# Even and odd partitions for attention's q and k loads, later counted times for the delta rule's loads, and six other order weights

## The chip, the cores and the metric

The kernel runs on one core of one Trainium2 chip. The metric is the device time of one launch in microseconds (us), the median of several runs; a profile is one more execution with the hardware profiler on. TensorE is called PE below, VectorE DVE, ScalarE ACT, GpSimd POOL, and SyncE, which issues all the transfers spoken of here, SP.

## The reference, cut to what matters

One layer of a mixer: 1024 latent tokens and 256 context tokens of width 1024 are normalised, projected once by a wide matrix, and go through two branches. Branch A is a gated delta rule over chunks, in both directions of the sequence, with 8 heads; branch B is differential softmax attention with 8 heads, each with two score maps. Both are gated, projected, merged and projected again.

```python
def gdn_chunk_scan(q, k, v, g, beta, s0, with_out):
    ...
    def step(s, xs_i):
        u_i, w_i, kd_i, gl_i = xs_i[:4]
        v_new = u_i - jnp.einsum('bhck,bhkv->bhcv', w_i, s)
        s_next = s * jnp.exp(gl_i)[..., None, None] + jnp.einsum('bhck,bhcv->bhkv', kd_i, v_new)
        if with_out:
            qd_i, qk_i = xs_i[4:]
            o = jnp.einsum('bhck,bhkv->bhcv', qd_i, s) + jnp.einsum('bhij,bhjv->bhiv', qk_i, v_new)
            return s_next, o
    ...

def diff_attend(q, k, v, lam):
    ...
    def block(qi):
        s = jnp.einsum('bqhcd,bkhcd->bhcqk', qi, k).astype(jnp.float32) * scale
        p = jax.nn.softmax(s, axis=-1)
        attn = p[:, :, 0] - lam * p[:, :, 1]
        return jnp.einsum('bhqk,bkhv->bqhv', attn.astype(v.dtype), v)
    ...

def mixer_output(...):
    ...
    merged = g_a * (y_a.reshape(b, length, GDN_WIDTH) @ w_oa) + g_b * (y_b.reshape(b, length, DIFF_V_WIDTH) @ w_ob)
    return merged @ w_out
```

## The kernel before, in words

**Stages.** By the span of the profile: modulation and the normalised input (0 to about 150 us); the input projection with the convolution and the delta rule's triangular matrices (to about 745 us); the scan of the delta rule, with the rest of the projection between its steps (to about 1290 us); a short stretch in which the projection ends and attention begins (to about 1345 us); attention, with the product by `w_oa` in its gaps (to about 1790 us); then the product by `w_ob`, the merge and `w_out`.

**How the order is set.** All work is written as generators, called streams here. Each yields the engine of its next instruction, the time counted for it, what it depends on, and the call that emits it. When the kernel is built, `flow` and `turn_flow` keep a counted clock for each engine, and emit the instruction that by these clocks could start first; in attention a number for each kind of stream, the table `ABIAS`, decides among those that could start within `TOL` = 0.02 us of each other on one engine, and the scores, the turns, the value products and the merge also have counted due times (`due`). What is emitted first stands first in its engine's queue, so the counted times fix the order on all five engines; on the chip each engine goes through its queue in that order, and waits where an input is not there. `later(t, us)` adds microseconds to the counted time of a finished item and emits nothing.

**The scan.** For each head h of 8 and each direction d of 2, ten tiles of 128 tokens (two chunks each) are gone through one after the other. A step has the products `chain` (with `vv`, or with `S,sk` for the state S; with `r,x`; with `vd,kk`) and two products `out`. `sets` loads four tiles for each head, on SP: `vv`, `kk`, `sk` and `sq` (512 to 640 KB each). `loads` fetches `x` for two steps at a time (256 KB), and POOL masks half of it (`tqk`). Between the steps stand `mm` (products of the input projection, 128x512), `gram` and the small triangular products `pz`, `pu`.

**Attention.** For each head, `att_load_ops` loads `qh` (high part of q) and `kk`, and `att_low_ops` loads `ql` (low part of q). Each of these tiles has 128 partitions by 2 rows; the 128 partitions are filled by two transfers, s = 0 and s = 1, of 64 partitions each, and `kk`'s two come from two different arrays (`kd[0]`, `kd[1]`). The scores `s` contract over the partitions, so that q and k have to agree on which partition holds what, and nothing else does. For each block of 128 queries, 64 in all: `s` is 12 products (`s<-kk,qh`, `s<-kk,ql`) into banks that DVE empties (`S`, L1560) with a running minimum; ACT takes the exponential (L1573); POOL and ACT scale and add the two maps (L1592, L1590, L1597); PE turns the map, ten transposes `t<-ct,S` (L63) in groups of 4, 4 and 2; ACT and DVE split what was turned into a high and a low part (`ah` L1629, `al` L1634), and empty the banks with that; PE multiplies by the values (`v<-ah,vh` and so on, 30 products of 256 columns for two blocks). `osq`, `oT` and `rr` belong to the head's norm; `rr<-rbd` comes back through memory before POOL (L1720) can scale `oT`. `merge` is the stream of the products `ma` (128x512), 16 groups of 24; each group's end is multiplied by a gate `g` (L1806), which SP loads ahead (`g<-gt`, L1791).

SP issues its transfers in its own queue's order, and the transfers share the core's DMA engines. All of PE's products have line L56, its transposes L63.

Of the kernel before, what the change touches and what calls it, by code (L numbers as in the profile page):

```python
# [8 lines left out]
F32 = mybir.dt.float32  # L9
# [8 lines left out]
P = 128  # L18
# [16 lines left out]
PE, DVE, ACT, POOL, DMA, ADMA, DV2, PL1 = range(8)  # L35
# [8 lines left out]
class Block:  # L44
# [193 lines left out]
    def front(self, st, early, kv0):  # L238
# [190 lines left out]
        for g, b in ((loads(), 0), (modulation(), 1), (smalls(), 1), (rms(), 2), (weights(), 1.5), (turns(), 1), (self.forever(turnq[0]), 1.2),  # L429
                     (self.forever(turnq[1]), 1.2), (main(), 9)):  # L430
            self.stream(g, b)
# [822 lines left out]
    def sets(self):  # L1254

        nc = self.nc
        free = []
        for h in range(H):
            yield lambda: self.gs and min(self.scanned) >= h and self.tailed >= h - 1
            w = dict(seen={}, oa=self.gs.tile([P, NL, P], F32, tag=f"oa{h % 2}", name="oa"))  # L1260
            free = [self.over, self.ready[h - 1]["tail"] if h else None]
            for n, src in (("vv", self.gv[h]), ("kk", self.gkk[h]), ("sk", self.gkq[h][:, :LT]), ("sq", self.gkq[h][:, LT:])):
                if h == 0 and n == "kk":
                    yield lambda: all((d, 0, 8) in self.units_ for d in range(2))
                w[n] = self.gs.tile([P, L] if n == "sq" else [P, NT, P] if n in ("kk", "vv") else [P, LT], F32, tag=n, name=n)
                w["t" + n] = yield DMA, 1.82, free, lambda: nc.sync.dma_start(
                    w[n], src.rearrange("(c p) f -> p c f", p=P) if n in ("kk", "vv") else src)
            self.ready[h] = w

    def loads(self, d):  # L1270

        nc, i = self.nc, 0
        order = ((8, 0, 2, 4, 6), (8, 6, 4, 2, 0))[d]
        for h in range(H):
            for c in order:
                yield lambda: self.gs and self.stored > h and len(self.used_[d]) > i - 2
                x, e = self.gs.tile([P, 2, 2, P], F32, tag=f"x{d}", name="x", bufs=2), 2 if c < NL else 1
                u = dict(x=x[:, 0], qk=x[:, 1])
                u["tx"] = yield DMA, 0.45 * e, [self.store_t[h], self.used_[d][i - 2] if i > 1 else None], \
                    lambda: nc.sync.dma_start(x[:, :e], self.xq[h][:, d, c // 2, :e])  # L1280
                if c < NL:
                    u["tqk"] = yield POOL, 0.72, [self.later(u["tx"], 1.0)], lambda: nc.gpsimd.tensor_tensor(
                        x[:, 1], x[:, 1], (self.up, self.lo)[d].unsqueeze(1).to_broadcast([P, 2, P]), ALU.mult)
                self.units_[d, h, c] = u
                i += 1
# [145 lines left out]
    def named(self, n, gen):  # L1431
        s = self.entry[n] = [gen, self.ABIAS.get(n, 0), None, None]
        s[2] = next(gen, None)
        self.streams.append(s)

    def due(self, n, i):

        self.entry[n][1] = self.ABIAS.get(n, 0) + self.DUE * i

# [48 lines left out]
    def att_load_ops(self, h):  # L1488

        q, pool, tags = self.nc.sync, self.a0 if h % 2 else self.gh[0], ("qh", "kk") if h % 2 else ("kq", "X")  # L1490
        w = self.aT[h] = dict(qh=pool.tile([P, 2, L], F32R, tag=tags[0], name="qh"),
                              kk=pool.tile([P, 2, LT], F32R, tag=tags[1], name="kk"))
        old = self.seen_.get(h - 2)
        w["t"] = []
        for s in range(2):
            d, v = slice(64 * s, 64 * s + 64), lambda x: x.rearrange("(c d) n -> d c n", c=2)
            w["t"] += [(yield DMA, 1.46, [old], lambda: q.dma_start(w["qh"][d].bitcast(F32), v(self.qd[0, h]))),
                       (yield DMA, 1.82, [old], lambda: q.dma_start(w["kk"][d].bitcast(F32), v(self.kd[s, h])))]

    def att_low_ops(self, h):  # L1500

        w = self.aT[h]
        w["ql"] = self.a0.tile([P, 2, L], F32R, tag=f"ql{h % 2}", name="ql")
        w["tl"] = []
        for s in range(2):
            w["tl"].append((yield DMA, 1.46, [self.seen_.get(h - 2)], lambda: self.nc.sync.dma_start(
                w["ql"][64 * s:64 * s + 64].bitcast(F32), self.qd[1, h].rearrange("(c d) n -> d c n", c=2))))

    def att_heads(self):
        for h in range(H):  # L1510
# [219 lines left out]
    def side_start(self):  # L1730
# [10 lines left out]
    ONACT = (1, 2, 3)  # L1741
    TOL = 0.02
    PACE = 4.48
    ABIAS = dict(rels=-0.59, softs=8.84, norms=5.82, gateq=-27.29, sums=-14.54,
                 outs=-42.85, lows=-2.4, highs=-9.33, adds=26.02, scales=31.0, evs=22.29, mouts=-3.31,
                 att_out=8.18, turns=3.19, scores=-12.11, merge=1.0)
    KEEP = 3

    def side_values(self):
# [453 lines left out]
```

## Time and profile before

| | |
|---|---|
| runs before | 1964.64, 1964.72, 1966.32 us; median 1964.72 |
| the profiled execution | 1966.57 us, of which the span is 1964.8 us |
| PE busy | 1909.4 us, 97% of the span |
| DVE, ACT, POOL busy | 75%, 54%, 34% |
| PE busy in the scan, 745 to 1290 us | 530.3 of 545 us |
| PE busy in the start of attention, 1290 to 1400 us | 102.4 of 110 us |
| PE busy in attention, 1400 to 1790 us | 383.0 of 390 us; DVE 333.5, ACT 304.3 |

Busy time on PE says that PE had a matmul in flight, not that it ran at its best rate. PEclk is the granted clock of PE, 1.00 at full rate. A view of waits names, for each engine, what ended a stretch in which it had nothing to do; a view by windows gives the busy time of each engine, the granted clock and the DMA engines' busy share in stretches of the span. The chain of waits goes back from the last instruction to whatever released each one.

### The profile page before, as it was taken

The numbers are of one execution on the slowest core, as the hardware profiler recorded it, in microseconds if no ns is written. First come the engines' busy times: TensorE is split into PE (matmuls) and PEld (weight loads), VectorE is DVE, ScalarE is ACT, GpSimd is POOL, SyncE is SP. The second block draws the span as 40 slices with busy tenths as digits, with TensorE's granted clock in tenths as the row PEclk, the third lists the DMA queues.
The fourth block names the chain that finished last, engine by engine and source line by source line (L and its number), as shares of the span: only waits on it lengthen the run. The fifth ranks groups of instructions, "written<-read, shape, count | busy, mean of one in ns | idle before, by whom it ended". The sixth has DMA issues, their size and how long they took to land.

```text
span 1964.8 us, 37491 instructions
## 1 busy us (share of the span) xinstructions
PE 1909.4 (97%) x13807; PEld 1679.4 (85%) x13807; DVE 1465.1 (75%) x3613; ACT 1069.4 (54%) x2191; POOL 677.4 (34%) x610
## 2 busy tenths in 40 slices
PE   6999999999999999999999999999999999999999
PEld 4988888899999998888888888877888888888887
DVE  4687998948877987778777673336688979895677
ACT  4543445335325464767755745456687868884222
POOL 3200000005431332343433234233666757762203
PEclk9999999999999999999999999999999999999999
DMA  9144544674546557866777466585566684426542
GB/s 329 60 132 107 144 94 114 145 220 140 183 132 211 150 191 207 257 208 211 249 217 248 114 221 214 153 202 159 159 161 151 156 230 132 129 87 209 182 155 86
DMA packets 383038, 336.39 MB, mean 171 GB/s; under 512 B 142609, under 2 KB 323443, under 8 KB 381831
## 3 DMA queue, kind: packets, MB, share of 16 engines
q1 hardware_dynamic: 382855, 333.99, 57.4%
q8 instruction: 109, 1.79, 0.4%
q14 instruction: 74, 0.61, 0.1%
HBM read 222.14 MB, written 111.79 MB: 170 GB/s over the span
## 4 chain that ended last, share of the span: by engine, by line
PE 77%; DVE 8%; DMA 7%; ACT 3%; issue 2%; SPq 1%; POOL 1%; DVEq 0%; ACTq 0%; POOLq 0%
PE mm L56 38%; PE s L56 6%; PE v L56 6%; PE chain L56 5%; PE mb L56 5%; PE ma L56 4%; PE x L56 3%; PE t L63 3%; PE out L56 2%; DVE S L1560 1%; PE gram L56 1%; DMA vv<-gv 1%; DVE ac L595 1%; PE pz L56 1%; DMA g<-gt 1%
## 5 line engine op out<-in xcount | busy, mean ns | idle before, releaser
L56 PE MATMUL mm<-hs,wh 128*128 128x512 f32 (+1 forms) x2048 | 648.2, 390 | 1.5 <-DVE hs L408 1.4
L56 PEld LDWEIGHTS mm<-hs,wh 128*128 128x128 f32 x2048 | 371.9, 190 | 60.8 <-issue 2.7
L56 PE MATMUL mm<-hs,wl 128*128 128x512 f32 (+1 forms) x1024 | 398.4, 389 | 1.1 <-issue 1.1
L56 PE MATMUL mm<-wh,hs 128*128 128x256 f32 (+1 forms) x1792 | 332.7, 286 | 0.3 <-ACT sq L977 0.3
L56 PEld LDWEIGHTS mm<-wh,hs 128*128 128x128 f32 x1792 | 280.7, 191 | 0.8 <-ACT sq L977 0.5
L1560 DVE TENSOR_SCALAR_CACHE_REDUCE S<-s,rsq 128x512 f32<-128x512 f32 (+1 forms) x384 | 241.4, 656 | 29.4 <-PE s L56 25.9
L56 PE MATMUL mm<-wl,hs 128*128 128x256 f32 (+1 forms) x896 | 255.6, 285 | 0.0
L56 PEld LDWEIGHTS mm<-hs,wl 128*128 128x128 f32 x1024 | 194.4, 190 | 28.7 <-issue 0.9
L1597 POOL TENSOR_TENSOR S<-S 128x1280 f32<-128x1280 f32 x64 | 188.6, 2954 | 78.0 <-ACT S L1590 77.1
L1573 ACT ACTIVATE S<-S,mn 128x1280 f32<-128x1280 f32 x128 | 175.3, 1371 | 44.9 <-DVE mn L1572 43.2
L56 PEld LDWEIGHTS mm<-wl,hs 128*128 128x128 f32 x896 | 171.3, 191 | 0.1
L595 DVE SCALAR_TENSOR_TENSOR ac<-xc,convT,ac 128x1284 f32<-128x1284 f32 (+1 forms) x96 | 138.8, 1449 | 11.9 <-ACT ac L593 11.2
L56 PE MATMUL s<-kk,qh 128*128 128x512 f32 (+1 forms) x384 | 144.5, 376 | 2.9 <-DVE S L1560 2.9
L56 PE MATMUL s<-kk,ql 128*128 128x512 f32 (+1 forms) x384 | 134.0, 359 | 2.5 <-DMA ql<-qd 2.5
L1634 DVE TENSOR_TENSOR al<-t,ah 128x512 fp32r<-128x512 f32 (+1 forms) x192 | 109.5, 596 | 29.8 <-ACT ah L1629 28.9
L1629 ACT CAST ah<-t 128x512 fp32r<-128x512 f32 (+1 forms) x192 | 91.9, 518 | 32.6 <-PE t L63 15.3
L580 POOL MEMSET xc<- 128x2 f32 (+1 forms) x64 | 3.6, 101 | 297.8 <-ACT sq L629 113.6
L63 PE MATMUL t<-ct,S 128*128 128x128 f32 x640 | 98.6, 277 | 4.1 <-DVE al L1634 2.6
L1157 DVE TENSOR_TENSOR ts<-ts,tmp 80x31 f32<-80x31 f32 (+15 forms) x248 | 97.5, 393 | 6.1
L1318 ACT ACTIVATE vd<-chain,edk 128x128 f32<-128x128 f32 x144 | 52.3, 370 | 89.2 <-PE chain L56 83.7
L1155 DVE TENSOR_TENSOR tmp<-ab,ts 80x31 f32<-80x31 f32 (+15 forms) x248 | 94.5, 381 | 8.5 <-DMA ab<-da 3.0
L56 PE MATMUL v<-ah,vh 128*128 128x256 f32 x320 | 93.0, 291 | 0.0
(296 smaller groups left out, 4338.3 us busy)
## 6 DMA issues: line engine op xcount, KB each, us to landing
wr<-in_w_in_dram SPq DMA_DIRECT2D x48, 512.0 KB, 6.0
hx<-in_w_in_dram SPq DMA_DIRECT2D x64, 256.0 KB, 6.4
x<-xq SPq DMA_DIRECT2D x64, 256.0 KB, 3.8
X<-gcd SPq DMA_DIRECT2D x8, 1280.0 KB, 8.3
kd<-col SPq DMA_DIRECT2D x40, 256.0 KB, 2.2
xq<-X SPq DMA_DIRECT2D x16, 640.0 KB, 7.4
kk<-kd SPq DMA_DIRECT2D x16, 640.0 KB, 7.9
kq<-gkq SPq DMA_DIRECT2D x8, 1152.0 KB
```

The source lines that it names most:

```text
L56: self.nc.tensor.matmul(out, lhsT, rhs, start=start, stop=stop)
L63: self.nc.tensor.transpose(out, src, self.ident[:src.shape[0], :src.shape[0]])
L580: x["e"].append((yield PL1, 0.1, [old], lambda: nc.gpsimd.memset(xc[:, a:b], 0.0)))
L595: t = yield DV2, 1.21e-3 * wd, [t], lambda: nc.vector.scalar_tensor_tensor(ac[:, :wd], xc[:, j:j + wd], self.convw(j, x["ct"]), ac[:, :wd] ...
L1155: t = yield DV2, n * w / 960.0 + 0.08, [t if j else self.later(t, 2.5), t1], lambda: V.tensor_tensor(tv, ab[:, j + 1:, j:j + 1].to_broadca ...
L1157: t = yield DV2, n * w / 960.0 + 0.08, [t, t1], lambda: V.tensor_tensor(ts[:, j + 1:, :w], ts[:, j + 1:, :w], tv, ALU.subtract)
L1318: td = yield ACT, 0.251, [t], lambda: nc.scalar.activation(vd, pc[:, 1], AF.Copy, scale=self.edk[:, c, g:g + 1])
L1560: e = yield DVE, 0.675 if m == 512 else 0.408, [e, self.sfree[c].get(n - 4 + c)], lambda: self.nc.vector.tensor_scalar(x["S"][c][:, o:o + ...
L1573: x["x"].append((yield ACT, 1.36, [e], lambda: nc.scalar.activation(S, S, AF.Exp, bias=x["mn"][:, c:c + 1], scale=-1.0, accum_out=w["l0"][ ...
L1597: e = yield POOL, 2.9, [e], lambda: self.nc.gpsimd.tensor_tensor(S0, S0, S1, ALU.add)
L1629: e = yield ACT, 0.48 if nb == 4 else 0.27, [t, y["old", k]], lambda: self.nc.scalar.copy(y["ah", k][:, :, q], pv)
L1634: t = yield DVE, 0.603 if k < 2 else 0.322, [e, y["old", k]], lambda: self.nc.vector.tensor_tensor(y["al", k][:, :, q], pv, y["ah", k][:, ...
```

## The change

It has three parts. (1) `att_load_ops` and `att_low_ops`: the two transfers of `qh`, `kk` and `ql` write the even partitions (s = 0) and the odd ones (s = 1), where before they wrote partitions 0 to 63 and 64 to 127. The number of transfers, their sizes and what is read from memory stay. (2) `sets` counts the end of each of its four loads 1.3 us later, and `loads` counts the end of each `x` load 1.0 us later for all who use it (before, for the mask on POOL alone). (3) Six numbers of the table `ABIAS` are other ones. Parts 2 and 3 emit nothing; they and the redrawn counted clocks put the same instructions into another order, from about 745 us of the span on. Before that place, and in the products by `w_ob` and `w_out`, PE's order is the one of before.

```diff
@@ sets @@
                 w["t" + n] = yield DMA, 1.82, free, lambda: nc.sync.dma_start(
                     w[n], src.rearrange("(c p) f -> p c f", p=P) if n in ("kk", "vv") else src)
+                w["t" + n] = self.later(w["t" + n], 1.3)
             self.ready[h] = w
@@ loads @@
                 u["tx"] = yield DMA, 0.45 * e, [self.store_t[h], self.used_[d][i - 2] if i > 1 else None], \
                     lambda: nc.sync.dma_start(x[:, :e], self.xq[h][:, d, c // 2, :e])
+                u["tx"] = self.later(u["tx"], 1.0)
                 if c < NL:
-                    u["tqk"] = yield POOL, 0.72, [self.later(u["tx"], 1.0)], lambda: nc.gpsimd.tensor_tensor(
+                    u["tqk"] = yield POOL, 0.72, [u["tx"]], lambda: nc.gpsimd.tensor_tensor(
@@ att_load_ops @@
         for s in range(2):
-            d, v = slice(64 * s, 64 * s + 64), lambda x: x.rearrange("(c d) n -> d c n", c=2)
+            d, v = slice(s, P, 2), lambda x: x.rearrange("(c d) n -> d c n", c=2)
@@ att_low_ops @@
             w["tl"].append((yield DMA, 1.46, [self.seen_.get(h - 2)], lambda: self.nc.sync.dma_start(
-                w["ql"][64 * s:64 * s + 64].bitcast(F32), self.qd[1, h].rearrange("(c d) n -> d c n", c=2))))
+                w["ql"][s:P:2].bitcast(F32), self.qd[1, h].rearrange("(c d) n -> d c n", c=2))))
@@ weights @@
-    ABIAS = dict(rels=-0.59, softs=8.84, norms=5.82, gateq=-27.29, sums=-14.54,
-                 outs=-42.85, lows=-2.4, highs=-9.33, adds=26.02, scales=31.0, evs=22.29, mouts=-3.31,
-                 att_out=8.18, turns=3.19, scores=-12.11, merge=1.0)
+    ABIAS = dict(rels=-0.59, softs=8.84, norms=5.82, gateq=-27.29, sums=-18.71,
+                 outs=-21.73, lows=-2.4, highs=-9.33, adds=36.19, scales=31.0, evs=22.29, mouts=-3.31,
+                 att_out=1.9, turns=3.19, scores=-21.22, merge=25.46)
```

The order moves at three places that matter below. The first is PE at the first head of the scan: `gram` is a product of the keys and queries, `mm` one of the input projection, and `chain<-vv,x` the first step of a head, which needs the load `vv`. Before:

```order
L56 MATMUL gram<-kq 128x128 x4
L56 MATMUL mm<-hs,wl 128x512
L56 MATMUL mm<-hs,wh 128x512 x2
L56 MATMUL mm<-hs,wl 128x512
L56 MATMUL chain<-vv,x 128x128 x2
L56 MATMUL mm<-hs,wh 128x512 x2
```

The same place in the changed kernel:

```order
L56 MATMUL gram<-kq 128x128 x4
L56 MATMUL mm<-hs,wl 128x512
L56 MATMUL mm<-hs,wh 128x512 x2
L56 MATMUL mm<-hs,wl 128x512
L56 MATMUL mm<-hs,wh 128x512 x2
L56 MATMUL mm<-hs,wl 128x512
L56 MATMUL mm<-hs,wh 128x512 x2
L56 MATMUL mm<-hs,wl 128x512
L56 MATMUL chain<-vv,x 128x128 x2
L56 MATMUL gram<-kq 128x128 x4
L56 MATMUL mm<-hs,wh 128x512 x2
L56 MATMUL chain<-vd,kk 128x128 x2
```

Six `mm` more stand ahead of the first `chain<-vv,x`, and four `gram` and two `mm` between it and `chain<-vd,kk`.

The second place is SP's queue at the first `ql` loads of attention, between the last weight tiles of the projection (`hx`), the gates' store (`gt<-zo`) and the values (`vh`, `vl`). Before:

```order
L1405 DMA ya<-oa 128x512
L880 DMA hx<-in_w_in_dram 128x4x128 x2
L1506 DMA ql<-qd 64x2x1024 x2
L1525 DMA vh<-vd 128x4x128
L1525 DMA vl<-vd 128x4x128
```

The same place in the changed kernel:

```order
L1407 DMA ya<-oa 128x512
L1508 DMA ql<-qd 64x2x1024
L880 DMA hx<-in_w_in_dram 128x4x128 x2
L1038 DMA gt<-zo 128x1024
L1508 DMA ql<-qd 64x2x1024
L1527 DMA vh<-vd 128x4x128
L1527 DMA vl<-vd 128x4x128
```

The first of the two `ql` transfers stands ahead of the two `hx` loads now, and the second behind a `gt<-zo` store.

The third place is PE early in attention, where transposes (`t`), scores (`s`), value products (`v`) and the merge (`ma`) take turns. Before:

```order
L56 MATMUL ma<-y,wl 128x512
L63 MATMUL t<-ct,S 128x128 x2
L56 MATMUL s<-kk,qh 128x512
L56 MATMUL s<-kk,ql 128x512
L56 MATMUL s<-kk,qh 128x512
L56 MATMUL s<-kk,ql 128x512
L56 MATMUL s<-kk,qh 128x256
L56 MATMUL s<-kk,ql 128x256
L63 MATMUL t<-ct,S 128x128 x8
L56 MATMUL s<-kk,qh 128x512
L56 MATMUL s<-kk,ql 128x512
L63 MATMUL t<-ct,S 128x128 x2
```

In the changed kernel, after as many scores or a few more:

```order
L56 MATMUL ma<-y,wh 128x512
L63 MATMUL t<-ct,S 128x128 x4
L56 MATMUL ma<-y,wh 128x512
L63 MATMUL t<-ct,S 128x128 x6
L56 MATMUL ma<-y,wl 128x512
L56 MATMUL s<-kk,qh 128x512
L56 MATMUL s<-kk,ql 128x512
L56 MATMUL s<-kk,qh 128x256
L56 MATMUL s<-kk,ql 128x256
L56 MATMUL ma<-y,wh 128x512 x2
```

The products `ma`, which stood in bursts of 24 early in attention, stand one or two at a time now, and the ten transposes of a block come in fewer pieces: over all of attention 160 runs of `t` become 98, of which 34 are the whole ten.

## The prediction

> **What bounds the kernel now.** I read the page's busy times first, then the stages by windows, then PE's waits, then the places of the long waits in the timeline, with clock and transfers there.
>
> ```profile
> span 1964.8 us, 37491 instructions
> PE 1909.4 (97%) x13807; PEld 1679.4 (85%) x13807; DVE 1465.1 (75%) x3613; ACT 1069.4 (54%) x2191; POOL 677.4 (34%) x610
> ```
> ```profile
> core 0: us, PE busy (x) PEld busy (x) DVE busy (x) ACT busy (x) POOL busy (x), PEclk, DMA share, GB/s
> 745.00:1290.00 545.00, 530.30 (x4648) 459.83 (x4647) 360.13 (x1028) 326.39 (x952) 188.65 (x246) 1.00 0.67 209
> 1345.00:1400.00 55.00, 49.97 (x288) 42.95 (x286) 39.75 (x136) 38.75 (x62) 30.16 (x14) 0.94 0.71 192
> 1400.00:1790.00 390.00, 382.98 (x2513) 338.27 (x2513) 333.51 (x1106) 304.30 (x515) 253.78 (x130) 1.00 0.55 151
> ```
>
> PE bounds every stage, with the others under 86%. PE's work is the same in both kernels, instruction for instruction, so the change can only act on PE's idle time, its clock, and what one product costs behind another. Between 745 and 1790 us PE waits for these (total, times, longest):
>
> ```profile
> PE s L56 <- DVE S L1560: 2.9, 6, 1.9
> PE v L56 <- DVE oT L1671: 2.6, 4, 1.0
> PE t L63 <- DVE al L1634: 2.6, 3, 1.8
> PE s L56 <- DMA ql<-qd: 2.5, 1, 2.5
> PE chain L56 <- DMA vv<-gv: 2.2, 4, 1.1
> PE chain L56 <- DMA x<-xq: 1.8, 1, 1.8
> PE chain L56 <- ACT vn L1322: 1.6, 1, 1.6
> PE chain L56 <- DMA sk<-gkq: 1.6, 1, 1.6
> PE t L63 <- POOL S L1597: 1.4, 1, 1.4
> PE chain L56 <- DMA kk<-gkk: 0.7, 2, 0.5
> ```
>
> No wait is longer than 2.5 us, but the longest cost more than they last. Four of them reach 1.8 us:
>
> ```profile
> 1150.07 0.46 PE L56 MATMUL chain<-vv,x 128*128 128x128 f32 x2 [1.83 <-DMA x<-xq]
> 1300.28 0.50 PE L56 MATMUL s<-kk,ql 128*128 128x512 f32 x1 [2.53 <-DMA ql<-qd]
> 1347.15 0.44 PE L63 MATMUL t<-ct,S 128*128 128x128 f32 x2 [1.76 <-DVE al L1634]
> 1388.47 0.39 PE L56 MATMUL s<-kk,qh 128*128 128x256 f32 x1 [1.89 <-DVE S L1560]
> ```
> ```profile
> 1151.10:1154.50 3.40, 3.40 (x12) 2.83 (x11) 1.58 (x3) 1.92 (x4) 3.07 (x4) 0.50 0.60 198
> 1301.30:1304.70 3.40, 3.40 (x10) 2.68 (x9) 2.52 (x8) 0.00 (x0) 0.00 (x0) 0.50 1.13 354
> 1349.10:1352.50 3.40, 3.40 (x17) 3.35 (x17) 2.74 (x10) 0.89 (x2) 0.00 (x0) 0.50 1.01 349
> 1390.00:1393.40 3.40, 3.40 (x16) 3.21 (x16) 3.12 (x12) 2.50 (x4) 0.76 (x2) 0.51 0.79 204
> ```
>
> About 2 us behind each, the granted clock is 0.50 for 3.4 us, which is 1.7 us of lost work. No such stretch follows the 1.6 us waits for `vn` and `sk`. So a wait of 1.8 us or more is priced at its length plus 1.7.
>
> [...]
>
> **The weights (part 3).** They join transposes and products of one kind. What a change of kind costs:
>
> ```profile
> 1418.94 0.60 PE L63 MATMUL t<-ct,S 128*128 128x128 f32 x4
> 1419.30 0.48 PE L56 MATMUL ma<-y,wh 128*128 128x512 f32 x1
> 1419.61 0.39 PE L56 MATMUL ma<-y,wl 128*128 128x512 f32 x1
> 1419.84 0.40 PE L56 MATMUL s<-kk,qh 128*128 128x512 f32 x1
> ```
>
> The first wide product behind transposes takes 1419.61 − 1419.30 = 0.31 us to the next start, an ordinary one 0.23, 0.08 less. By the two orders such places are 178 before and 138 after in attention, 335 and 347 in the scan: −40 + 12 = −28, 2.2 us gained. Bounds 0 and 3.2, the second if the scan's twelve cost nothing.
>
> At the start of attention the second block's transposes waited for `al`, because `ah` of the block waited for a store of the projection's last gate:
>
> ```profile
> 1341.97 1.35 PE L63 MATMUL t<-ct,S 128*128 128x128 f32 x10
> 1346.26 1.73 ACT L1629 CAST ah<-t 128x256 fp32r<-128x256 f32 x4 [2.31 <-DMA gt<-zo]
> ```
>
> The new order has twelve `s` between the same two blocks of ten, and ACT still does that gate and an exponential ahead of `ah`. I leave this wait, 1.8 + 1.7, where it is: term 0, between −3.5 and +3.5 (twice the wait, if the lost `mm` cover shows).
>
> **The loads at head changes (part 2).** The scan's waits for loads stand at the first steps of heads, where the counted time is too early. With 1.3 us more counted for `vv`, `kk` and `sk`, products `mm` are put ahead: six at the first head. The longest `vv` and `kk` waits were 1.1 and 0.5 us, so I take both sums away (2.2 and 0.7); `sk` keeps 1.6 − 1.3 = 0.3, which saves 1.3; `x` is counted 1.0 later and keeps 0.8 of 1.8, which saves 1.0, and its clock drop goes, 1.7. Sum 6.9. From below it is 0, if the real loads slide with the order; from above, with `sk` and `x` whole, 6.3 + 1.7 = 8.0. I take 6.9, since the loads are issued on SP, where no product stands. The `mm` for this come from the end of the projection: 136 of the 5760 `mm` follow the first `s` before, 60 after. If that cover is missing, the start of attention pays, which is in the bounds of the term above.
>
> **The partitions (part 1).** Transfers into 128 partitions and into 64 can be told apart at the same busy share of the DMA engines:
>
> ```profile
> 1350.00:1355.00 5.00, 5.00 (x30) 4.80 (x29) 3.86 (x15) 1.52 (x3) 0.00 (x0) 0.75 1.04 393
> 1375.00:1380.00 5.00, 5.00 (x24) 4.12 (x23) 1.76 (x7) 3.88 (x5) 2.38 (x1) 1.00 1.04 205
> DMA to landing us min/median/max: 8.7/15.4/15.9
> ```
>
> In the first row `y<-ya`, 128 partitions, moves at 393 GB/s; in the second a head's q and k loads, 64 at a time, at 205, with the engines just as busy. The third row is of `ql`, in the view of that tile. One half-tile thus reaches half of what the core can write. Even partitions lie spread over the whole height, and if the limit goes with where partitions lie, they come at up to 393. A head's six loads are 4 x 512 + 2 x 640 KB = 3.41 MB (2 MiB of q and 1.25 MiB of k): 16.6 us at 205 GB/s, 8.7 at 393. Three waits hang on this.
>
> First, `ql` of head 0. It landed 8.7 us after issue, and PE waited 2.5 for it. At the faster rate it saves some 4.1 us, more than the wait: 2.5 + 1.7 = 4.2 gone. If the rate stays, only the order helps: six `mm` more stand between the last `oT` transposes and the first `s`, 6 x 0.23 = 1.4 us, but the second `ql` is now behind `gt<-zo`, which waits on ACT; I put that case at 0.7, half of it. I take 4.2.
>
> Second, the gate of the first merge group:
>
> ```profile
> 1372.01 0.50 SPq L1791 DMA_DIRECT2D g<-gt  x1
> 1387.32 0.69 DVE L1806 TENSOR_TENSOR g<-ma,g 128x512 f32<-128x512 f32 x1 [2.53 <-DMA g<-gt]
> 1387.93 0.48 DVE L1560 TENSOR_SCALAR_CACHE_REDUCE S<-s,rsq 128x256 f32<-128x256 f32 x1
> ```
>
> It was issued right behind a head's six loads and came 15.3 us later. DVE stood 2.53 us for it with `S` queued behind, and PE's `s` waited 1.89 for that `S`. With loads some 8 us shorter `g` is there in time, and the first group ends later too (after 77 pieces of `s`, where it was 54). Gone: 1.89 + 1.7 = 3.6. From below 0, if another transfer takes its place.
>
> Third, `rr`, again behind a head's loads:
>
> ```profile
> 1600.13 0.60 SPq L1717 DMA_DIRECT2D rr<-rbd  x1
> 1618.78 2.83 POOL L1720 TENSOR_TENSOR oT<-oT,rr 128x256 f32<-128x256 f32 x4 [12.21 <-DMA rr<-rbd]
> 1631.08 0.44 PE L63 MATMUL t<-ct,S 128*128 128x128 f32 x2 [1.35 <-POOL S L1597]
> ```
>
> POOL stood 12.2 us, and its later sum `S` then held a transpose for 1.35. Between 0 and 1.4 of this goes; the order there is redrawn, so I take half, 0.7.
>
> **New waits.** A new order on all engines makes waits as well as removing them. As a price for what is not seen I take what the old order has of such chance waits: `s` for `S` and `vn`, 1.9 + 1.6, and one clock drop of 1.7, 5.2 us; between 0 and twice that.
>
> **The sum.** 2.2 + 0 + 6.9 + 4.2 + 3.6 + 0.7 = 17.6 less 5.2 is 12.4 us. The profiled execution took 1966.57 us, 1.8 of it outside its span, so 1954.2; it stood 1.85 above the median, so **1952** as a median. Its own range: all terms but that at the start of attention at their upper ends and no new waits, 3.2 + 8.0 + 4.2 + 3.6 + 1.4 = 20.4, gives 1944; twice the new waits gives 1958.
>
> **The rivals.** *The waits only move.* Each wait at a head change stands for a load that comes late because its tile came free late; one filled, the next item of the chain waits instead. For it: the chain waited 1.6 us for `vn` too, with no load in it. Against it: the `g` and `ql` waits hang on bytes. Then only the 2.2 us of joined products stay: 1962.5.
>
> *The loads don't get faster.* Two transfers of 64 partitions each, and the limit is in each transfer, or in memory reads, and not in where the partitions lie. For it: nothing in this trace has a transfer into every other partition. Against it: 393 and 205 at the same share. Then `ql` gives 0.7, `g` half (1.8, by the later end of its group), `rr` nothing: 2.2 + 6.9 + 0.7 + 1.8 − 5.2 = 6.4, so 1958. [...]
>
> *Blocks of ten cost banks (slower).* The transposes of a block go into three banks, which `ah` on ACT and then `al` on DVE free. In runs of four and six between other products a bank has time to come free; 34 of the 64 blocks are one run of ten now. If each block then waited for the bank, 0.19 us a block (12.4 / 64) uses up the gain, and at 0.4 us, 25.6 in all, the time is 1978. For it: ACT and DVE are busy 304 and 334 of 390 us, so the freeing is late easily, and the wait of 1.76 above is such a one. Against it: all `t` waits of the old order make 4.0 us over 640 transposes, and the ten at 1341.97 ran in one piece.
>
> **Chances.** The forecast 0.60, waits that only move 0.17, loads no faster 0.10, banks 0.13. About 0.2%, 3.9 us, is what a measurement of this kernel can tell from no change; below 1960.8 is faster. The forecast is faster but for 0.02, the loads' case but for 0.01, the waits' case 0.05 of its 0.17: faster 0.72, same 0.15, slower 0.13. The range takes in the two milder rivals above, to 1966 with some loss on top, and below 1944 the 2.6 us of `v` for `oT`, which the new weights could also free: 1942 to 1966.
>
> **What would show it.** Right: 350 GB/s or more in the stretches of q and k loads; no `s` wait for `ql`, no DVE wait of microseconds for `g`; the clock at 0.50 behind one or two waits, not four; scan waits for `vv` and `kk` near nothing. Wrong: q and k loads still at 205; `t` waits for `al` of over 10 us in attention; waits of `chain` for `r`, `S` or `vn` that grow by what the loads' waits lose. A second thing would make me wrong: a stall at the start of attention over 5 us, where 76 `mm` are missing.

## The result, and the profile after

| | us | ratio to the kernel before, 95% interval |
|---|---|---|
| before | 1965.52 (median of 4) | |
| changed | 1942.28 (median of 4, 1941.70 to 1943.38) | 0.9882 [0.9865, 0.9899] |
| forecast | 1952, range 1942 to 1966 | |

The change is 23.2 us faster, where 12.7 were forecast; the time lies at the low end of the range. The profiled execution took 1943.38 us with a span of 1941.5, against 1966.57 and 1964.8. The page of the changed kernel:

```profile
span 1941.5 us, 37467 instructions
PE 1901.2 (98%) x13807; PEld 1675.8 (86%) x13807; DVE 1451.9 (75%) x3613; ACT 1065.9 (55%) x2191; POOL 679.2 (35%) x610
```

Its windows, in the stretches that were shown of before:

```profile
745.00:1290.00 545.00, 541.32 (x4721) 471.90 (x4720) 350.53 (x1029) 326.40 (x957) 191.81 (x247) 1.00 0.67 211
1345.00:1400.00 55.00, 54.14 (x357) 47.98 (x356) 49.50 (x175) 46.39 (x79) 40.78 (x20) 1.00 0.46 149
1400.00:1790.00 390.00, 385.04 (x2447) 337.61 (x2446) 318.61 (x1033) 290.91 (x488) 240.67 (x126) 1.00 0.47 157
```

In the scan PE is idle 3.7 us of 545 where it was 14.7. And PE's waits from 745 to 1790 us (total, times, longest), down to 0.4 us in total; two more, of `v` for `al` and for `oT`, are 0.3 and 0.2 us:

```profile
PE t L63 <- DVE al L1636: 2.1, 1, 2.1
PE ma L56 <- DVE g L1808: 1.9, 2, 1.1
PE s L56 <- DVE S L1562: 1.7, 5, 0.5
PE t L63 <- ACT zo L1036: 1.7, 1, 1.7
PE p L56 <- DVE Z L1177: 1.4, 1, 1.4
PE mm L56 <- POOL wl L885: 1.0, 1, 1.0
PE m L63 <- DVE g L1808: 0.8, 1, 0.8
PE chain L56 <- DVE r L1311: 0.4, 1, 0.4
PE chain L56 <- DVE S L1331: 0.4, 1, 0.4
```

No wait for a load is left in this profile: `vv`, `kk`, `sk`, `x` and `ql` are all gone, and so are the chain's waits for `vn`, and nearly all for `r` and `S`. Of the four stretches between 745 and 1790 us with the clock at half there is one, behind the wait for `al`:

```profile
1331.10:1334.50 3.40, 3.40 (x14) 3.02 (x13) 2.82 (x7) 3.38 (x6) 0.00 (x0) 0.50 1.02 375
```

The loads of q and k run at 354 GB/s where they ran at 205; the second row is `ql`'s landing, from its tile's view:

```profile
1352.00:1357.00 5.00, 4.75 (x29) 3.99 (x28) 4.98 (x17) 5.00 (x10) 1.02 (x1) 1.00 1.01 354
DMA to landing us min/median/max: 4.0/8.1/9.0
```

The gate of the first merge group is multiplied without a wait (before it had 2.53 us in brackets):

```profile
1383.22 0.69 DVE L1808 TENSOR_TENSOR g<-ma,g 128x512 f32<-128x512 f32 x1
```

**Where the 23.3 us of span went.** PE's waits in 745 to 1790 us are 28.4 us in sum before and 11.9 after: 16.5. Three half-clock stretches fewer, 1.7 us each: 5.1. What is left is 1.7 us, near the 2.2 of the joined products. By PE's idle time in windows, up to the same place in both kernels (29.3 us in 745 to 1790 before, 13.7 in 745 to 1767 after), the first term is 15.6 and what is left 2.6. This last term is by difference, and no run isolates it.

### The profile page after: what moved, and what is told of

It reads as the page before. It is cut to its first block, busy times and chain, and to the rows that moved or that the text cites. A ratio compares the mean times of both kernels' runs of the same rounds, so it can differ in the third digit from the quotient of the medians.

```text
span 1941.5 us, 37467 instructions
## 1 busy us (share of the span) xinstructions
PE 1901.2 (98%) x13807; PEld 1675.8 (86%) x13807; DVE 1451.9 (75%) x3613; ACT 1065.9 (55%) x2191; POOL 679.2 (35%) x610
## 4 chain that ended last, share of the span: by engine, by line
PE 83%; DVE 6%; DMA 4%; ACT 3%; issue 2%; SPq 1%; POOL 1%; DVEq 0%; ACTq 0%; POOLq 0%
PE mm L56 42%; PE s L56 6%; PE v L56 5%; PE chain L56 5%; PE mb L56 5%; PE ma L56 4%; PE x L56 3%; PE t L63 3%; PE out L56 3%; DVE S L1562 1%; PE gram L56 1%; DVE ac L595 1%; PE tr L63 1%; PE pz L56 1%; PE mp L56 1%
## 5 line engine op out<-in xcount | busy, mean ns | idle before, releaser
L56 PE MATMUL ma<-y,wh 128*128 128x512 f32 x256 | 93.3, 410 | 1.9 <-DVE g L1808 1.9
L1631 ACT CAST ah<-t 128x512 fp32r<-128x512 f32 (+1 forms) x192 | 87.8, 520 | 9.3 <-PE t L63 8.9
L56 PE MATMUL v<-al,vh 128*128 128x256 f32 x320 | 90.7, 284 | 0.4 <-DVE al L1636 0.3
```

The lines of the kernel that those rows point to most:

```text
L56: self.nc.tensor.matmul(out, lhsT, rhs, start=start, stop=stop)
L1631: e = yield ACT, 0.48 if nb == 4 else 0.27, [t, y["old", k]], lambda: self.nc.scalar.copy(y["ah", k][:, :, q], pv)
```

## The experiments

Three parts, so the first six runs do each part alone and each pair. P stands for the partitions, L for the later counted times, W for the six weights. All times are compared as ratios to the kernel before on the same chip. The last columns are from the trace of each run: scan is from the start of the first `gram` to that of the first `s`, attention from there to the last `v`. The scan in this sense takes in the part of the projection from 447 us on. Some orders leave 136 products `mm` behind the first `s`, others 60, so each `mm` above 60 is counted as 0.23 us of the scan and not of attention. The last column counts windows of 3.4 us with the clock at half, from 745 to 1790 us.

| | median us | ratio [95%] | scan, us | attention, us | half-clock windows |
|---|---|---|---|---|---|
| before | 1965.5 | | 867.3 | 470.2 | 4 |
| P | 1952.67 | 0.9939 [0.9922, 0.9955] | 863.4 | 460.3 | 0 (and one at 599 us) |
| L | 1963.08 | 0.9991 [0.998, 1.0002] | 855.4 | 479.1 | 5 (in four stretches) |
| W | 1962.01 | 0.9986 [0.9973, 0.9998] | 865.7 | 466.7 | 2 |
| L and W | 1951.36 | 0.9926 [0.9913, 0.994] | 852.1 | 466.6 | 1 |
| P and L | 1949.68 | 0.9933 [0.992, 0.9946] | 850.5 | 468.6 | 1 |
| P and W | 1955.44 | 0.9965 [0.9952, 0.9978] | 864.9 | 460.3 | 2 |
| changed (P, L, W) | 1942.28 | 0.9882 [0.9865, 0.9899] | 851.0 | 463.2 | 1 |

### The partitions alone

```diff
-            d, v = slice(64 * s, 64 * s + 64), lambda x: x.rearrange("(c d) n -> d c n", c=2)
+            d, v = slice(s, P, 2), lambda x: x.rearrange("(c d) n -> d c n", c=2)
...
-                w["ql"][64 * s:64 * s + 64].bitcast(F32), self.qd[1, h].rearrange("(c d) n -> d c n", c=2))))
+                w["ql"][s:P:2].bitcast(F32), self.qd[1, h].rearrange("(c d) n -> d c n", c=2))))
```

> The kernel before with the even and odd partitions alone; the order on all engines stays that of before, so that only the loads' speed differs. By the waits: the scores' wait for ql goes (2.5 us and a clock drop of 1.7), the gate's g is there in time and the scores' wait for S with it (1.9 + 1.7), half of the transposes' wait for POOL (0.7): 8.5 us, 1957.0 us. By the rival that the order is what counts and the loads alone are hidden: within 3.9 us of 1965.5. Three clock drops fall to one at the start of attention and one in the scan.

Measured: 12.0 us by the ratio (9 to 15). The first rows of PE's waits from 745 us on, and further down those for `S`:

```profile
PE v L56 <- DVE oT L1671: 2.6, 4, 1.0
PE t L63 <- DVE al L1634: 2.6, 3, 1.8
PE chain L56 <- DVE S L1331: 1.9, 3, 0.8
PE chain L56 <- DMA x<-xq: 1.8, 1, 1.8
PE chain L56 <- DMA vv<-gv: 1.6, 2, 0.8
...
PE s L56 <- DVE S L1560: 1.0, 5, 0.2
```

The waits for `ql` (0.3 us left) and of the scores for `S` behind `g` are gone, the chain's waits in the scan stay. This is the price foreseen, 8.5 us, on an order that did not change. From 745 us on the clock never fell in this execution, though `x` and `al` were waited for 1.8 us each, and so two stretches of 1.7 more were saved than forecast. One stretch came in that the profile of before does not have, at 599 us, ahead of all that the change touches:

```profile
599.40:602.80 3.40, 3.40 (x19) 3.40 (x18) 3.27 (x8) 0.75 (x2) 0.00 (x0) 0.50 0.00 0
```

That makes 8.5 + 3.4 − 1.7 = 10.2 us, inside the interval. What these traces show of where the clock falls stands at the end.

### The later counted times alone

```diff
+                w["t" + n] = self.later(w["t" + n], 1.3)
...
+                u["tx"] = self.later(u["tx"], 1.0)
-                    u["tqk"] = yield POOL, 0.72, [self.later(u["tx"], 1.0)], lambda: nc.gpsimd.tensor_tensor(
+                    u["tqk"] = yield POOL, 0.72, [u["tx"]], lambda: nc.gpsimd.tensor_tensor(
```

> The kernel before with the later counted times alone (half loads and weights of before). By the prediction's term: the chain's waits for vv, kk, sk and x shrink, 6.9 us, 1958.6 us. By the profile after, where the chain waits for r, S and vn went with them (11.4 us of chain waits and one clock drop of 1.7, less some 0.9 for eleven more changes from a narrow product to a wide one): 12.2 us, 1953.3 us. By the rival that waits only move: above 1962. The wait for ql stays 2 us or more, with its clock drop.

Measured: 1.8 us, with an interval that reaches no change. Of the three expectations only the number of the rival, above 1962 us, was met. The first two were wrong for the whole, and the second was near for the scan alone (12.2 us): it is 11.9 us shorter (867.3 to 855.4). Attention is 8.9 us longer and gives most of it back. The half-clock stretches are four again, and the first of them lasts two windows, 6.8 us. The wait for `ql`, expected at 2 us or more with a clock drop, is 1.5 us without one. The first of PE's waits from 745 us on:

```profile
PE s L56 <- DVE S L1562: 5.1, 9, 3.3
PE v L56 <- DVE oT L1673: 3.3, 7, 1.0
PE out L56 <- ACT vn L1324: 3.2, 1, 3.2
PE m L63 <- POOL bry L179: 2.8, 1, 2.8
PE t L63 <- DVE al L1636: 2.1, 1, 2.1
```

Three of them lead back to transfers that stand behind a head's half loads on SP. For the 3.3 us, ACT stood 7 us for the merge's weights `wq`, with an exponential queued behind; for the 2.8, POOL stood for `rr`, with `bry` behind:

```profile
1375.01 0.62 ACT L1778 CAST wh<-wq 128x512 fp32r<-128x512 f32 x1 [7.05 <-DMA wq<-in_w_oa_dram]
1674.22 0.74 POOL L1722 TENSOR_TENSOR oT<-oT,rr 128x256 f32<-128x256 f32 x1 [12.75 <-DMA rr<-rbd]
```

### The weights alone

```diff
-    ABIAS = dict(rels=-0.59, softs=8.84, norms=5.82, gateq=-27.29, sums=-14.54,
-                 outs=-42.85, lows=-2.4, highs=-9.33, adds=26.02, scales=31.0, evs=22.29, mouts=-3.31,
-                 att_out=8.18, turns=3.19, scores=-12.11, merge=1.0)
+    ABIAS = dict(rels=-0.59, softs=8.84, norms=5.82, gateq=-27.29, sums=-18.71,
+                 outs=-21.73, lows=-2.4, highs=-9.33, adds=36.19, scales=31.0, evs=22.29, mouts=-3.31,
+                 att_out=1.9, turns=3.19, scores=-21.22, merge=25.46)
```

> The kernel before with the six other weights alone. The scan is that of before. If the weights only join products: thirty changes from a narrow product to a wide one fewer in attention, 0.08 us each, 2.4 us, 1963.1 us. If the later end of the first merge group also takes away the wait for g: 3.6 us more, 1959.5 us. If they carry most of the gain: below 1955. If blocks of ten cost banks, the transposes' waits for al grow to over 10 us and the time is above 1966.

Measured: 2.8 us (0.4 to 5.3). That fits the joined products, and does not tell them from a part of the wait for `g`. Nor from the clock: the profile has two half-clock windows fewer than before, 3.4 us, and one of the two is missing behind a wait for `x` that is longer than before (2.3 us). The transposes wait for `al` once, 1.8 us, so the rival of banks falls: the blocks of ten don't cost what was feared.

### The partitions undone

```diff
-            d, v = slice(s, P, 2), lambda x: x.rearrange("(c d) n -> d c n", c=2)
+            d, v = slice(64 * s, 64 * s + 64), lambda x: x.rearrange("(c d) n -> d c n", c=2)
...
-                w["ql"][s:P:2].bitcast(F32), self.qd[1, h].rearrange("(c d) n -> d c n", c=2))))
+                w["ql"][64 * s:64 * s + 64].bitcast(F32), self.qd[1, h].rearrange("(c d) n -> d c n", c=2))))
```

> The changed kernel with the loads into halves of the partitions again; its order on all engines stays that of the changed kernel. If the weights had already taken the wait for g away, the loads give ql and half of rr, 4.9 us, so 1947.2 us; if both hang on the loads, 8.5 us, 1950.8 us. If the redrawn order needs the fast loads (q and k are asked for later in it), more waits for q and k show, and the time is above 1953.

Measured: 1951.36 us, 0.9926 where the changed kernel has 0.9882, so the partitions are worth some 8.7 us on the new order too. The order on all five engines is that of the changed kernel, which makes it a clean pair for the loads. The partitions leave the order alone in the other pairs as well: by the ratios, each good to some 3 us, they are worth 12.0 us on the kernel before, 11.4 beside L, 4.1 beside W and 8.7 beside both. In the windows, in the tile view of `ql`, and on POOL and ACT:

```profile
1356.00:1361.00 5.00, 5.00 (x33) 4.42 (x32) 5.00 (x17) 4.86 (x7) 2.98 (x2) 1.00 1.03 207
DMA to landing us min/median/max: 5.2/15.8/17.2
1482.23 2.13 POOL L1722 TENSOR_TENSOR oT<-oT,rr 128x256 f32<-128x256 f32 x3 [11.80 <-DMA rr<-rbd]
1270.57 0.62 ACT L884 CAST wh<-hx 128x512 fp32r<-128x512 f32 x1 [4.25 <-DMA hx<-in_w_in_dram]
1271.41 0.49 PE L56 MATMUL out<-vn,x 128*128 128x128 f32 x2 [2.64 <-ACT vn L1324]
```

The same POOL instruction of the changed kernel:

```profile
1470.94 2.12 POOL L1722 TENSOR_TENSOR oT<-oT,rr 128x256 f32<-128x256 f32 x3 [5.10 <-DMA rr<-rbd]
```

So 207 GB/s against 354 at about the same busy share of the DMA engines (1.03 and 1.01), and what stands behind the loads on SP comes later: `rr` in attention by about 7 us, and at about 1255 us, where the first head's q and k are loaded under the scan, the projection's last weights `hx`. For these ACT stood 4.25 us with `vn` queued behind, and PE's `out` 2.64. That place was in no term of the prediction. The loads of 64 partitions each can be fast: with a step of two they run at 354 GB/s, side by side at 207, with the same bytes and in the same order. In this pair the rate goes with which partitions a transfer fills, and not with how many; by what way is in no trace.

The time is near the second expectation (8.5 us, 1950.8), but this trace does not show the two waits behind it. The first merge group's `g` is in time here as well, and the scores wait 1.7 us for `S` as in the changed kernel, so the new order had taken that wait away without the loads. What came back is `out` for `vn` 2.6, `v` for `ah` 1.3 and `ql` 1.0; in all PE waits 16.1 us from 745 to 1790 us, where the changed kernel waits 11.9. These 4.2 us are most of the difference of the two spans (1946.1 and 1941.5). The profiled execution was the fastest of the six, and where the others lost some 3 us more no trace shows.

### Partitions and later times; partitions and weights

```diff
-    ABIAS = dict(rels=-0.59, softs=8.84, norms=5.82, gateq=-27.29, sums=-18.71,
-                 outs=-21.73, lows=-2.4, highs=-9.33, adds=36.19, scales=31.0, evs=22.29, mouts=-3.31,
-                 att_out=1.9, turns=3.19, scores=-21.22, merge=25.46)
+    ABIAS = dict(rels=-0.59, softs=8.84, norms=5.82, gateq=-27.29, sums=-14.54,
+                 outs=-42.85, lows=-2.4, highs=-9.33, adds=26.02, scales=31.0, evs=22.29, mouts=-3.31,
+                 att_out=8.18, turns=3.19, scores=-12.11, merge=1.0)
```

> The changed kernel with the weights of before, that is partitions and later counted times. In the run with the later times alone, half loads were ahead of four long PE waits: ACT stood for hx (out waits 3.2 us for vn), the scores waited 3.3 for S and 1.5 for ql, a transpose m 2.8 for POOL, which stood 12.8 us for rr; with three clock drops of 1.7 these are 15.8 us. If the slow loads made them, they go and the time is 1947 us, and the weights give 5 us of the changed kernel's gain. If the two parts only add (12.1 and 1.7 us), it is 1951. If the order that the old weights draw makes these waits whatever the loads, it stays above 1955.

Measured: 0.9933, 13.2 us, which is about what P and L alone add up to (13.8). The order is that of the run with L alone, and the four long waits there are gone (attention 479.1 to 468.6), which settles that the slow loads made them. But attention is still 8.3 us longer than with P alone, at 468.6 against 460.3; 1.7 of it is one half-clock window. PE's waits from 1290 us on:

```profile
PE v L56 <- DVE oT L1673: 3.3, 7, 1.0
PE s L56 <- DVE S L1562: 2.3, 10, 0.3
PE t L63 <- DVE al L1636: 2.1, 1, 2.1
PE t L63 <- ACT zo L1036: 1.7, 1, 1.7
PE ma L56 <- DVE g L1808: 1.6, 2, 0.8
PE t L63 <- POOL S L1599: 0.9, 2, 0.5
```

Two kinds: many short waits, likely those of an order drawn anew under weights that were chosen for another one, and the waits for `zo` and `al` at the start of attention. With the new weights on top (the changed kernel) attention is 5.4 us shorter again: the `v` waits for `oT` fall from 3.3 to 0.2.

The other pair leaves out the later times:

```diff
-                w["t" + n] = self.later(w["t" + n], 1.3)
...
-                u["tx"] = self.later(u["tx"], 1.0)
```

> The changed kernel without the later counted times. The scan is that of before, with its 12 us of chain waits (0.8 in the changed kernel) less some 2 that the even and odd loads take away. If the later times are worth what the scan shows once the loads are fast, 9 to 10 us: 1952 us. If they are worth what they gave alone, 1.7 us: 1944. The clock drops once or twice, by where the waits fall.

Measured: 0.9965, 6.9 us, some 5 less than the partitions alone gave by the ratios of two chips. The later times are thus worth 16 us here by the ratios (0.9965 to 0.9882), more than either expectation. The stages of the two profiles of P don't show a loss of 5 us: scan and attention agree within 1.5 us, and two half-clock windows stand against the one at 599 us. Attention has its shortest time here (460.3, as with P alone), and the scan is 13.9 us longer than in the changed kernel. So the scan's gain from the later times is 11.9, 12.9, 13.6 and 13.9 us in the four pairs that differ by them alone; without the half-clock windows that fell into the scan it is 13.6, 11.2, 13.6 and 10.5. The chain's waits make 8.5 to 10.4 us of it. Without the later times the weights give attention 3.5 us with half loads (470.2 to 466.7) and nothing with fast ones (460.3 both times), with them 12.5 and 5.4 us. The likely reading is that what they mainly do is to fit attention to where the scan now ends; no run shows it by itself.

### Which of the later times, and how much

```diff
-                w["t" + n] = self.later(w["t" + n], 1.3)
+                w["t" + n] = self.later(w["t" + n], 1.6)
```

> The changed kernel with vv, kk, sk and sq counted 1.6 us later, not 1.3. The chain's waits for loads are gone already, so nothing can be gained there: by the waits 1942 within 2 us. If a redrawn order costs or gives by chance as much as the prediction allowed for new waits (5.2 us), the time leaves 1942 by 3 us or more, and the place is in attention.

Measured: 1942.41 us, 0.9892. The order differs from the first head on, and nothing came of it: scan 852.1 and attention 461.2 us. A redrawn order alone moved the time by less than can be told here.

```diff
-                u["tx"] = self.later(u["tx"], 1.0)
                 if c < NL:
-                    u["tqk"] = yield POOL, 0.72, [u["tx"]], lambda: nc.gpsimd.tensor_tensor(
+                    u["tqk"] = yield POOL, 0.72, [self.later(u["tx"], 1.0)], lambda: nc.gpsimd.tensor_tensor(
```

> The changed kernel with only the four loads of a head counted later; x is counted as before (1.0 later for the mask alone). If each count takes away its own load's wait and nothing else, x keeps 1.8 us and perhaps its clock drop of 1.7: 2 to 4 us above the changed kernel on the same chip. If the waits for r, S and vn, which hold no load, went by these four counts too, the scan's other waits stay below 5 us. If they went by the x counts, they come back, and the time is 8 us or more above.

Measured: 1946.49 us, 4.0 above the changed kernel beside it (1942.46). That is at the edge of the first expectation (2 to 4 us), but not by its way: PE waits for no `x` in this profile, though `x` is counted as before. The sign of the second, other waits of the scan below 5 us, is there, as the rows below show. Three half-clock windows stand against one, 3.4 us, one of them behind a wait of 2.7 us ahead of a triangular product `p`. What the later `x` is worth in itself is not shown. And the counterpart:

```diff
-                w["t" + n] = self.later(w["t" + n], 1.3)
```

> The changed kernel with only x counted later for all its users; vv, kk, sk and sq as before. By own waits: vv 2.2, kk 0.7, sk 1.3 come back, 4 us above the changed kernel. If the chain's waits for r, S and vn went because the four loads of a head pushed the whole head back: 8 to 12 us above. If any later count that draws the order anew is as good: within 3 us.

Measured: 1958.16 us, 15.7 above. The chain's waits tell the two apart. With only the four loads counted later:

```profile
PE chain L56 <- DVE r L1310: 1.9, 4, 0.8
...
PE chain L56 <- DMA sk<-gkq: 0.5, 1, 0.5
...
PE chain L56 <- ACT vd L1319: 0.3, 1, 0.3
PE chain L56 <- DVE S L1332: 0.2, 1, 0.2
```

With only `x` counted later:

```profile
PE chain L56 <- DMA kk<-gkk: 1.9, 2, 1.7
PE chain L56 <- DMA vv<-gv: 1.7, 2, 1.3
PE chain L56 <- DMA sk<-gkq: 1.7, 1, 1.7
PE chain L56 <- ACT vn L1323: 1.5, 1, 1.5
...
PE chain L56 <- DVE r L1310: 1.2, 2, 0.9
```

2.9 us of chain waits in the first (the four rows), 8.0 in the second (these five; 9.2 with two more). Not all of the 15.7 us is theirs: in the second PE also waited 6.6 us ahead of the triangular products `p` (2.7 in the first), which no expectation had, and whose cause was not followed; and its clock was at half for four windows, where the changed kernel has one, 5.1 us. The waits for `r`, `S` and `vn` go with the four loads of the head, though none of them holds a load. Where a head's first step stands later in PE's queue, its later steps stand later too, with more projection products between; that this spacing is what covers DVE and ACT there is the likely reading, and not shown by itself.

### The start of attention

In the changed kernel ACT goes through an exponential with its table load, then a table load and the projection's last gate `zo` (1.28 us for each of the two loads), and the transposes wait 1.7 us for it, then 2.1 for `al`. One more condition holds that exponential back:

```diff
-            yield lambda: len(x["e"][c]) == 3
+            yield lambda: len(x["e"][c]) == 3 and (self.open_ or x["n"] < 3)
```

> The changed kernel with one more condition: the exponential of the fourth block waits in the order until the projection's last gate (zo) is out. In the changed kernel ACT loads a table for one exponential and another for that gate, and the transposes wait 1.7 us for zo and 2.1 for al, with a clock drop of 1.7. If the tables are the cause, 2.6 us of loads go, and with them the wait for zo and the clock drop: 1938 to 1940. If the later exponentials are then what is late: 1942 or more.

Measured: 1940.22 us, 0.9886 [0.9871, 0.9902] on its chip. The profile has no wait of the transposes for `zo` or `al` and no half-clock window; 1.4 us for `mn` came in place. To see whether the chip made the difference, the changed kernel ran once more, beside the same condition with 1.6 us in place of 1.3:

> The changed kernel once more, on the chip of the two runs beside it: 20 to 23 us below the kernel before there. If the trial with the projection's last gate first was faster only by its chip, the next run shows no difference to this one.

> The changed kernel with the fourth block's exponential held back until the projection's last gate is out, and the four loads of a head counted 1.6 us later. If the table loads ahead of the gate cost PE its wait and the clock drop at the start of attention there too (1.7 and 1.7), 2 to 4 us below the changed kernel on the same chip. If the other order, with 27 projection products behind the first score in place of 60, has moved the place: within 1.5 us of it.

Measured: 1942.46 (0.989 [0.987, 0.991]) and 1943.13 us (0.989 [0.9872, 0.9909]). All four ratios lie within each other's intervals. The condition removes the wait it names, and no gain in time is shown.

## Why the prediction was right, and where it was off

**The direction and the mechanism** held: long waits and half clocks go, and PE's work stays. Put as waits, clock and products the sum is 16.5 + 5.1 + 1.7 = 23.3 us of span, where the prediction had 12.4. The time stands 0.3 us inside the range. The terms at their upper ends, but for that at the start of attention, gave 1944; that the range goes lower is owed to the `v` for `oT`, which fell from 2.6 to 0.2 us indeed. That the parts mis-sized below still end inside it is in part luck.

**Part 2 was mis-sized.** The term of 6.9 took away each load's own wait and its one clock drop. Measured in four pairs, the scan shortens by 12 to 14 us. The step that failed is the one that looked at loads alone: the chain's other waits were left standing, and `vn`, 1.6 us, was even part of the price for new waits. Two of them stand in the same view of before as the ten rows of the prediction, which left them out:

```profile
PE chain L56 <- DVE S L1331: 1.9, 3, 0.8
PE chain L56 <- DVE r L1309: 1.6, 2, 0.9
```

In the changed kernel the chain waits are 0.8 us in all, 12.0 before. The two runs with one kind of count each show that the four loads' counts move most of them, to 2.9 us, and the `x` counts few, to 9.2. The rival that waits only move was refuted for the scan; the run with L alone looks like it from outside, at 1.8 us, but there the scan's gain was made and lost again in attention.

**Part 1 was right** in its rate (393 at most, 354 measured, over 350 as asked) and, on the order of before, in its three waits: `ql` and `g` gone, and no transpose waits for POOL's `S` any more. In the changed kernel `rr` on POOL is down from 11.8 to 5.1 us in the same order, but `g` is in time with half loads too. The term, 8.5 us, stands against 12.0 alone and 8.7 on the new order; that the second comes so near is luck, since the waits that make it are others. The second `ql` behind the store `gt<-zo` cost nothing: it landed 9.0 us after issue at most, and the first score waits for nothing. The rival that loads don't get faster falls by the rows above.

**Part 3** was given 2.2 us for joined products. Its price holds: in attention of the changed kernel a product of 512 columns takes 0.316 us to the next start behind a product of 128 columns or fewer, and 0.232 behind a wider one (medians of 123 and 789). Alone the weights gave 2.8, beside the partitions alone no gain (by the ratios a loss of 5), beside the later times 10 to 13. The prediction took the parts as a sum; under the old weights the later times cost attention 8 to 9 us, likely because they shift where it begins, and the new weights mostly take that back. That this would be needed was not foreseen, and the size of the whole hangs on it: by ratios P, L and W alone give 12.0 + 1.8 + 2.8 = 16.6 us, together 23.2.

**The start of attention** kept its wait, as assumed: `al` 2.1 us with its clock drop, and `zo` 1.7 as a new one. **New waits**, priced at 5.2, are `zo` 1.7, `Z` 1.4, `wl` 1.0 and 0.6 more for `g`, 4.7 in all, with no clock drop of their own.

**The rival of banks** falls: one wait of 2.1 us for `al` and one of 1.7 for `zo` are all that the 34 blocks of ten show.

## What to carry to other kernels

Where two transfers fill one tile and the consumer doesn't care which partition holds what, a split into even and odd partitions is worth trying in place of halves: here q's and k's loads ran at 354 GB/s with it and at 205 without, the transfers stayed the same in number and size, and what stands behind them on the queue came sooner too, which was as much of the gain as the loads' own wait. In an order that is fixed by counted times, a load that was counted too early cost more than its own wait here, and the correction in one stage was worth its whole only with other weights in the next; parts of such a change should be judged together.

## What the runs showed of the hardware

**In these traces the half clock keeps to a grid.** The four stretches of before begin at 1151.10, 1301.25, 1349.05 and 1390.00 us by fine windows. Each lasts 3.4 us, and from the first to the last it is 238.90 us, 70 times 3.413. The distances between them are 44.0, 14.0 and 12.0 times 3.413 us; in the run with L alone 19.0, 13.0 and 89.0 times. With PE's idle time added up over windows of this grid, in all 14 traces from 150 to 1900 us, every window with 1.71 us or more was followed by one at half clock (1.71, 1.83, 1.85 and 2.40 us in before, 2.12 in the changed kernel). None with less than 1.3 us was, but for the first half of the double stretch with L alone, itself at half clock, with 1.0; between these it went either way (1.67 us in the changed kernel was not followed by one, 1.48 in the run with 1.6 us for the loads was), for a reason that is not shown. So a wait counts here by how much of it falls in one window. The run with the partitions undone has waits of 2.6 us (1271) and 2.1 us (1332), and the clock at 1.00 behind both:

```profile
1269.00:1277.00 8.00, 5.59 (x26) 4.69 (x27) 1.12 (x3) 4.80 (x19) 2.57 (x3) 1.00 0.45 141
1329.00:1340.00 11.00, 8.87 (x64) 7.98 (x64) 9.67 (x34) 8.14 (x15) 3.11 (x2) 1.00 0.99 343
```

The first is split 0.97 and 1.67 us over two windows. The instructions around 599 us, which no part of the change touches, show how executions differ: ahead of a product `p` there PE stood 0.6 us in before, 0.9 in the changed kernel, 1.8 with P alone and 1.9 in the run with 1.6 us for the loads, and the clock fell behind the last two. That the executions of one kernel spread by some multiples of 1.7 us would follow from it (this profiled execution took 1947.91 us, the other five 1950.1 to 1951.7), but the others have no trace that shows it. The prediction's 1.7 us for each wait from 1.8 on is therefore a price that falls due by chance.
